# A hybrid diffusion backbone on one core: the decays of its recurrent mixer computed as two exponentials of the tanh

## The chip, the cores and the metric

The kernel runs on 1 core of a Trainium2 chip. TensorE (PE in the rows; its weight load is PEld), VectorE (DVE), ScalarE (ACT), GpSimd (POOL) and SyncE (SP, here a queue for DMAs) each work through their own list of instructions in order and wait for one another through semaphores. The metric is the device time of one execution in microseconds; the median of several runs counts.

## What is computed

One layer over 256 context tokens and 1,024 latent tokens of 1,024 channels: a projection into many column groups, three mixers side by side (a recurrent one over 256 channels, neighbourhood attention over 512, a short gated convolution), an output projection, and an expert mixer that selects 128 of 16,384 rows for each token. The change lies in the recurrent mixer. For each of its two directions `d`:

```
w_raw = w0 + tanh(z_w) @ w_up
decay = exp(-exp(-softplus(-w_raw) - 0.5))          # = exp(-exp(-0.5) * sigmoid(w_raw))
a     = sigmoid(a0 + z_a @ a_up)
b     = kk * a
k_dir = k * (1 + (a - 1) * k_a)
S     = S * decay - (S kk) b^T + v k_dir^T           # token after token
y     = S r
...
out   = (groupnorm(y) * lnx + (sum(r * k * r_k)) * v) * gate
```

The sigmoid is formed from a tanh: sigmoid(x) = 0.5 + 0.5 tanh(x/2).

## The kernel before

The recurrence is worked in batches of 256 tokens, as four chunks of 64. `batch(step, d)` handles one batch of one direction; there are ten (step 0 to 4, both directions), and each has two halves `h` of 128 channels. So the lines inside `for h in range(2)` run 20 times. A half begins with the projection `wr` on TensorE (L498, L499), forms the decays `de` and their inverses `di` (L502 to L518), runs a running product over each chunk (`pe`, `pi`, L525 and L526), forms the key factors `nb` and `kd` (L530 to L532), multiplies them with the inverse decays on GpSimd (`bb`, `kb`, L541 and L542), and starts its matrix products (`p1`, `p2`, L554). Behind the two halves of a batch come a triangular solve (`lp`, `lt`, `lx`, L613 to L630) and the products over the four chunks (`mc`, `yc`, L661 to L680). In the last four batches that complete a group of tokens (`last`), the sum of both directions is normalised (L692 to L707), a bonus is added (`yd`, L713), and the result goes to DRAM as `d_y` (L718). The Ln and Exp of that normalisation stand in `rsqrt` (L136, L137).

The decays before are a chain: tanh on ScalarE, an affine form on VectorE, a second tanh `q`, its squares on ScalarE, three instructions on VectorE, and two products on GpSimd. With q = tanh of a quarter of the exponent, (1 + q)^2 and (1 - q)^2 times (1 + q^2)(1 + q^4)(1 + q^8) give the two exponentials.

A scheduler sets the order of instructions on each engine from the program order and a simulated time; the projections of the attention and convolution inputs (`pj`) and the attention of the first 256 tokens (`attend` with two blocks, L854) depend on nothing in the mixer and are laid between its batches. Tiles with one buffer (`th`, `x2`, `de` and others, tag and `bufs=1`) are reused by the next half, and 128x512 banks of PSUM with the tag `ra` rotate over three buffers. The stretch ends when the mixer's last batch, (4, 1), has written its `d_y`: `group(0, ...)` (L1211) reads it for the output projection.

Of the kernel before, what the change touches and what calls it, by code (L numbers as in the profile page):

```python
# [10 lines left out]
F32 = mybir.dt.float32  # L11
# [4 lines left out]
AF = mybir.ActivationFunctionType  # L16
OP = mybir.AluOpType
AX = mybir.AxisListType

P = 128  # L20
# [8 lines left out]
E05 = float(np.exp(np.float32(-0.5)))  # L29
# [24 lines left out]
def hybrid_kernel(ctx: ExitStack, tc: tile.TileContext, A: dict, out: bass.AP, dbg=None):  # L54
    nc = tc.nc
# [67 lines left out]
    def eps_tile(v):  # L123
        if v not in epst:
            epst[v] = const.tile([P, 1], F32, name=f"eps{len(epst)}")
            nc.vector.memset(epst[v], v)
        return epst[v]

    for v_ in (1e-6, 1e-12, 64e-5):
        eps_tile(v_)  # L130
# [154 lines left out]
    kat = cload("kat", [P, 2], A["rw_k_a"])  # L285
# [124 lines left out]
    cw = st_c.enter_context(pool("cw"))  # L410
# [7 lines left out]
    nc.vector.tensor_scalar_mul(hb[:, 0:4], w0t, 0.5)  # L418
    nc.vector.tensor_scalar_mul(hb[:, 4:8], a0t, 0.5)
    d1 = cw.tile([P, 4, 65], F32, name="d1")  # L420
    nc.vector.memset(d1, 0.0)
# [9 lines left out]
    gp = st_g.enter_context(pool("gp"))  # L431
# [17 lines left out]
    def v4(ap):  # L449
        return ap.rearrange("p (c t) -> p c t", t=64)  # L450
# [4 lines left out]
    def batch(step, d):  # L455
        g = 0 if step == 0 else (step if d == 0 else 5 - step)
        c0, t0, lat = 4 * g, 256 * g, g > 0
        last = g in seen
        if lat:
            seen.add(g)  # L460
        if last:
            bo = gp.tile([P, 2, 4], F32, tag="bo", name=f"bo{g}", bufs=2)
            tl = t0 - TC
        S = [None, None]
# [5 lines left out]
        for h in range(2):  # L470
            ci = 2 * d + h

            def gt(name, shape, bufs=1, h=h):
                return gp.tile(shape, F32, tag=name, name=f"{name}_{step}{d}{h}", bufs=bufs)
# [24 lines left out]
            nc.tensor.matmul(pw[:, 256:], aup[:, ci, :], lwt[:, 1, :], start=True, stop=True)  # L499
            th, q, at = gt("th", [P, 256]), gt("q", [P, 256]), gt("at", [P, 256])  # L500
            x2, x4 = gt("x2", [P, 256]), gt("x4", [P, 256])
            nc.scalar.activation(th, pw[:, :256], AF.Tanh, bias=hb[:, ci:ci + 1], scale=0.5)  # L502
            nc.scalar.activation(at, pw[:, 256:], AF.Tanh, bias=hb[:, 4 + ci:5 + ci], scale=0.5)
            nc.vector.tensor_scalar(th, th, -0.25 * E05, -0.25 * E05, op0=OP.mult, op1=OP.add)
            nc.scalar.activation(q, th, AF.Tanh)

            nc.scalar.activation(th, q, AF.Square)
            nc.scalar.activation(x2, th, AF.Square)
            nc.scalar.activation(x4, x2, AF.Square)
            nc.vector.tensor_scalar_add(x4, x4, 1.0)  # L510
            nc.vector.scalar_tensor_tensor(x2, x2, 1.0, x4, op0=OP.add, op1=OP.mult)
            nc.vector.scalar_tensor_tensor(x2, th, 1.0, x2, op0=OP.add, op1=OP.mult)
            nc.scalar.activation(th, q, AF.Square, bias=1.0)
            nc.scalar.activation(x4, q, AF.Square, bias=1.0, scale=-1.0)
            de, di = gt("de", [P, 4, 65]), gt("di", [P, 4, 65])
            for t_, o_ in ((th, de), (x4, di)):
                nc.gpsimd.memset(o_[:, :, 64 * d:64 * d + 1], 0.0)
                nc.gpsimd.tensor_mul(o_[:, :, 1 - d:65 - d], v4(t_), v4(x2))  # L518
            nc.vector.tensor_scalar(at, at, 0.5, 0.5, op0=OP.mult, op1=OP.add)
            at = v4(at)  # L520

# [6 lines left out]
            tot = pe[:, :, 64:65] if d == 0 else pe[:, :, 0:1]  # L528
            nb, kd = v4(gt("x2", [P, 256])), v4(gt("x4", [P, 256]))
            nc.vector.scalar_tensor_tensor(nb, kk, -1.0, at, op0=OP.mult, op1=OP.mult)  # L530
            nc.vector.tensor_scalar(kd, at, -1.0, kat[:, h:h + 1], op0=OP.add, op1=OP.mult)
            nc.vector.scalar_tensor_tensor(kd, kd, 1.0, kr_, op0=OP.add, op1=OP.mult)  # L532
            krd = gt("krd", [P, 4, 3, 64], 4)
# [34 lines left out]

            ex = v4(gt("q", [P, 256]))
            nc.vector.tensor_mul(ex, p1v[:, :, 1, :], cst[:, C_X0 if d == 0 else C_X1, 0:64].unsqueeze(1).to_broadcast([P, 4, 64]))  # L570
# [110 lines left out]
        if not lat:  # L681
            return
        y = gp.tile([P, 2, 4, 64], F32, tag="y", name=f"y{step}{d}", bufs=1)
        src = ych.rearrange("p (h c b) -> p h c b", h=2, c=4)
# [19 lines left out]
        nc.vector.tensor_reduce(va, y2, op=OP.add, axis=AX.X)  # L704
        rsqrt(gp, rs, va, 8, 64e-5, 1.0 / 64, "gn")
        nc.vector.tensor_mul(y, y, bc(rs))
        nc.vector.tensor_mul(y, y, lnx.unsqueeze(2).to_broadcast([P, 2, 4, 64]))  # L707
        for h in range(2):
            yd = rot("yd", [P, 4, P], 1)
            for a in range(2):  # L710
                q_ = slice(64 * a, 64 * a + 64)
                for u in range(4):
                    nc.vector.scalar_tensor_tensor(yd[q_, u, q_], S[h]["vS"][q_, u], bo[q_, h, u:u + 1], y[q_, h, u], op0=OP.mult, op1=OP.add)  # L713
            ps = bank(f"yo{h}{g}", "ch")
            for u in range(4):
                nc.tensor.matmul(ps[:, u * 64:(u + 1) * 64], yd[:, u, :], cst[:, C_STK, 0:64], start=True, stop=True)
            nc.vector.tensor_mul(gs[:, h, :], ps[:, :256], gs[:, h, :])
# [772 lines left out]
```

## Time and profile before

| | |
|---|---|
| median of 3 runs | 3760.8 us |
| the runs | 3756.59, 3760.8, 3775.57 us |
| the profiled execution's own time | 3766.3 us |
| its span in the trace | 3764.6 us |
| TensorE, busy share of the span | 90% |
| VectorE | 79% |
| ScalarE | 42% |
| GpSimd | 40% |
| first tanh of the mixer's decays (L502) | starts at 143.1 us |
| last write of the mixer's result (L718) | issued at 953.1 us |

The times are for the whole layer. The mixer stands between about 100 and 953 us; the rest of the span is the attention of the later tokens and the expert mixer. Shares over the span say little about this stretch, which has to be read by windows.

### The profile page before, as it was taken

The page shows a single profiled execution, that of the slowest core. Times are in us where ns is not written, and L with a number is a line of the kernel's source. Part 1 is how long each engine was busy: PE and PEld are TensorE (multiplying, and loading weights), DVE is VectorE, ACT ScalarE, POOL GpSimd, SP SyncE. Part 2 cuts the span into 40 slices and gives each one's busy share as a digit, 9 for nine tenths or more (in the row PEclk, how much of TensorE's full clock was granted, in tenths as well). Part 3 has the DMA queues.
Part 4 walks back from the last instruction along what each step waited for, and adds up shares of the span by engine and source line. Part 5 has one row for each costly group of instructions (what it writes and reads, how often), then busy time and mean ns, then how long its engine had stood idle before and what let it go on. Part 6 is the DMA issues. An engine that isn't in the chain of part 4 may idle for free.

```text
span 3764.6 us, 56051 instructions
## 1 busy us (share of the span) xinstructions
PE 3383.9 (90%) x19927; PEld 3052.6 (81%) x19927; DVE 2984.7 (79%) x6392; ACT 1587.2 (42%) x3084; POOL 1503.7 (40%) x1196
## 2 busy tenths in 40 slices
PE   7778888988779887989889999999996999999997
PEld 6567778887668766879889999999985888888886
DVE  6576757886595656978869999999876788888888
ACT  3543333442435433345343776666632333323332
POOL 2444443320044223355433425555451444444443
PEclk9889998998789888999999999999998999999998
DMA  6434534220565645698967879999998999999997
GB/s 245 138 94 147 167 114 121 70 61 22 159 205 171 205 146 174 242 322 295 326 232 263 301 253 358 351 361 357 340 367 272 314 356 348 344 347 333 338 355 244
DMA packets 405784, 928.09 MB, mean 247 GB/s; under 512 B 45568, under 2 KB 182144, under 8 KB 399872
## 3 DMA queue, kind: packets, MB, share of 16 engines
q1 hardware_dynamic: 248064, 408.81, 33.6%
q0 software_dynamic: 111920, 407.95, 30.1%
q10 hardware_dynamic: 45520, 107.76, 7.4%
q8 instruction: 157, 2.57, 0.3%
q14 instruction: 123, 1.01, 0.1%
HBM read 802.74 MB, written 121.63 MB: 246 GB/s over the span
## 4 chain that ended last, share of the span: by engine, by line
PE 39%; DVE 10%; issue 6%; DMA 4%; ACT 2%; POOL 1%; SPq 0%; DVEq 0%; ACTq 0%; POOLq 0%
PE ds L159 5%; PE ds L157 5%; PE ds L158 5%; PE dp L158 5%; PE dp L159 5%; PE dp L157 5%; DVE ru L1159 3%; PE gm L1074 3%; PE dq L157 2%; PE dq L159 2%; PE dq L158 2%; DMA rv<-in_peer_v_dram,idx 2%; DVE acc L1170 1%; DMA kd<-d_kn 1%; DVE ob L1066 1%
## 5 line engine op out<-in xcount | busy, mean ns | idle before, releaser
L1142 POOL DMA_INDIRECT ru<-in_peer_u_dram,idx x384 | 514.5, 1340 | 736.3 <-ACT dqs L1394 168.4
L1142 POOL DMA_INDIRECT rv<-in_peer_v_dram,idx x384 | 511.6, 1332 | 707.1 <-ACT dqs L1394 272.2
L1159 DVE CUSTOM_DVE_ANT_0 ru<-ru,h 128x1024 f32<-128x1024 f32 x384 | 475.7, 1254 | 82.4 <-DMA ru<-in_peer_u_dram,idx 80.2
L1170 DVE SCALAR_TENSOR_TENSOR acc<-rv,gw,acc 128x1024 f32<-128x1024 f32 x381 | 488.2, 1281 | 49.5 <-DMA rv<-in_peer_v_dram,idx 44.4
L158 PE MATMUL dp<-dvls,dwhs 128*128 128x512 f32 x896 | 348.2, 389 | 0.0
L159 PE MATMUL dp<-dvhs,dwls 128*128 128x512 f32 x896 | 346.1, 389 | 0.0
L157 PE MATMUL dp<-dvhs,dwhs 128*128 128x512 f32 x896 | 318.7, 394 | 4.7 <-ACT dvhs L1344 4.7
L207 POOL TENSOR_TENSOR wl<-w,wh 128x1024 fp32r<-128x1024 f32 x68 | 170.3, 2507 | 291.8 <-ACT wh L205 268.3
L157 PE MATMUL pj<-hbh,wh 128*128 128x512 f32 (+1 forms) x544 | 220.8, 407 | 24.8 <-ACT wh L205 15.9
L1276 ACT ACTIVATE ge<-ds 128x256 f32<-128x256 f32 (+1 forms) x256 | 110.8, 434 | 265.3 <-PE ds L159 224.4
L159 PE MATMUL pj<-hbh,wl 128*128 128x512 f32 (+1 forms) x544 | 215.7, 397 | 2.7 <-POOL wl L207 2.7
L158 PE MATMUL pj<-hbl,wh 128*128 128x512 f32 (+1 forms) x544 | 216.8, 399 | 0.8 <-POOL hbl L188 0.8
L1348 ACT CAST dwhs<-dws 128x640 fp32r<-128x640 f32 x128 | 91.6, 730 | 269.3 <-DVE dws L1347 141.6
L157 PEld LDWEIGHTS dp<-dvhs,dwhs 128*128 128x128 f32 x896 | 171.1, 191 | 40.8 <-ACT dvhs L1344 5.1
L158 PEld LDWEIGHTS dp<-dvls,dwhs 128*128 128x128 f32 x896 | 168.2, 188 | 34.9
L159 PEld LDWEIGHTS dp<-dvhs,dwls 128*128 128x128 f32 x896 | 168.2, 188 | 34.8
L157 PE MATMUL dq<-dvhs,dwhs 128*128 128x512 f32 x384 | 150.8, 393 | 31.5 <-ACT dvhs L1344 28.7
L1345 DVE TENSOR_TENSOR dvls<-dvs,dvhs 128x1024 fp32r<-128x1024 f32 x128 | 155.5, 1219 | 24.2 <-ACT dvhs L1344 23.8
L1344 ACT CAST dvhs<-dvs 128x1024 fp32r<-128x1024 f32 x128 | 133.0, 1051 | 76.5 <-DMA dvs<-in_peer_v_dram 76.4
L1074 PE MATMUL gm<-oa,ob 128*128 128x128 f32 x1280 | 158.2, 276 | 3.2 <-DVE oa L1061 1.9
L1394 ACT COPY dqs<-dq 128x512 f32<-128x512 f32 x90 | 52.8, 587 | 256.5 <-PE dq L159 256.5
L1074 PEld LDWEIGHTS gm<-oa,ob 128*128 128x128 f32 x1280 | 153.6, 193 | 4.2 <-issue 4.1
(1995 smaller groups left out, 10488.4 us busy)
## 6 DMA issues: line engine op xcount, KB each, us to landing
du<-in_peer_ut_dram SPq DMA_DIRECT2D x128, 512.0 KB
dvs<-in_peer_v_dram SPq DMA_DIRECT2D x128, 512.0 KB
d_ge<-ge ACTq DMA_DIRECT2D x128, 320.0 KB
d_g<-gt ACTq DMA_DIRECT2D x40, 1024.0 KB
dgs<-d_g SPq DMA_DIRECT2D x32, 1280.0 KB
dws<-d_ge SPq DMA_DIRECT2D x128, 320.0 KB
w<-in_w_in_dram SPq DMA_DIRECT2D x68, 512.0 KB
wq<-in_q_w_dram SPq DMA_DIRECT2D x48, 512.0 KB
```

Source lines behind the costliest of these rows:

```text
L157: nc.tensor.matmul(ps, lh_, rh_, start=start, stop=False)
L158: nc.tensor.matmul(ps, lh_, rl_, start=False, stop=False)
L159: nc.tensor.matmul(ps, ll_, rh_, start=False, stop=stop)
L207: WE[0].tensor_tensor(wl, w, wh.bitcast(F32), op=OP.subtract)
L1074: nc.tensor.matmul(ps[:, t * P:(t + 1) * P], ob[:, q + t], oa[:, q + t], start=True, stop=True)
L1142: paced(nc.gpsimd.indirect_dma_start(out=r, out_offset=None, in_=A[tab], in_offset=bass.IndirectOffsetOnAxis(ap=idx[:, tt, s:s + 1], axis=0)))
L1159: yield from rows("peer_u", tt, lambda s, u: nc.vector.tensor_tensor_reduce(u, u, h2, 1.0, 0.0, OP.mult, OP.add, act[:, s:s + 1]))
L1170: nc.vector.scalar_tensor_tensor(acc, v, w[:, s:s + 1], acc, op0=OP.mult, op1=OP.add)
L1276: ev = nc.scalar.activation(ge[:, t0:t0 + n], ps, AF.Gelu_apprx_tanh)
L1344: nc.scalar.copy(vh, v)
L1345: sv = nc.vector.tensor_tensor(vl, v, vh.bitcast(F32), op=OP.subtract)
L1348: nc.scalar.copy(wh, wt)
```

## The change

The decays become two exponentials of the first tanh: exp(-c) and exp(+c) with c = 0.5 exp(-0.5) (1 + tanh), each one ScalarE instruction that writes straight into `de` and `di`. The factor -a becomes one affine form on ScalarE (`nb`, from the tanh `at`), the factor 1 + (a - 1) k_a another (`kd`, with scale and bias per channel from the new small tile `kac`), and VectorE multiplies each with `kk` and `k`. The tile `q` is gone; the temporary `ex` takes the buffer of `th` instead. In the finishing batches the bonus product `vb` = v times its sum is formed before the normalised `y` is there, the reciprocal root comes from `rsqrt_few` (twelve small VectorE instructions, no table functions), and `yd` is a plain sum over four chunks at a time.

```diff
-    for v_ in (1e-6, 1e-12, 64e-5):
+    for v_ in (1e-6, 1e-12, 64e-5, -0.5 * E05, 0.5 * E05, -0.5):
         eps_tile(v_)
...
+    kac = cw.tile([P, 2, 2], F32, name="kac")
+    nc.vector.tensor_scalar_mul(kac[:, 0], kat, 0.5)
+    nc.vector.tensor_scalar(kac[:, 1], kat, -0.5, 1.0, op0=OP.mult, op1=OP.add)
...
-            th, q, at = gt("th", [P, 256]), gt("q", [P, 256]), gt("at", [P, 256])
-            x2, x4 = gt("x2", [P, 256]), gt("x4", [P, 256])
+            th, at = gt("th", [P, 256]), gt("at", [P, 256])
+            nb, kd = gt("x2", [P, 256]), gt("x4", [P, 256])
             nc.scalar.activation(th, pw[:, :256], AF.Tanh, bias=hb[:, ci:ci + 1], scale=0.5)
+            de, di = gt("de", [P, 4, 65]), gt("di", [P, 4, 65])
+            for sg, o_ in ((-1.0, de), (1.0, di)):
+                nc.gpsimd.memset(o_[:, :, 64 * d:64 * d + 1], 0.0)
+                nc.scalar.activation(o_[:, :, 1 - d:65 - d], v4(th), AF.Exp, bias=eps_tile(sg * 0.5 * E05), scale=sg * 0.5 * E05)
             nc.scalar.activation(at, pw[:, 256:], AF.Tanh, bias=hb[:, 4 + ci:5 + ci], scale=0.5)
-            nc.vector.tensor_scalar(th, th, -0.25 * E05, -0.25 * E05, op0=OP.mult, op1=OP.add)
-            nc.scalar.activation(q, th, AF.Tanh)
-
-            nc.scalar.activation(th, q, AF.Square)
-            nc.scalar.activation(x2, th, AF.Square)
-            nc.scalar.activation(x4, x2, AF.Square)
-            nc.vector.tensor_scalar_add(x4, x4, 1.0)
-            nc.vector.scalar_tensor_tensor(x2, x2, 1.0, x4, op0=OP.add, op1=OP.mult)
-            nc.vector.scalar_tensor_tensor(x2, th, 1.0, x2, op0=OP.add, op1=OP.mult)
-            nc.scalar.activation(th, q, AF.Square, bias=1.0)
-            nc.scalar.activation(x4, q, AF.Square, bias=1.0, scale=-1.0)
-            de, di = gt("de", [P, 4, 65]), gt("di", [P, 4, 65])
-            for t_, o_ in ((th, de), (x4, di)):
-                nc.gpsimd.memset(o_[:, :, 64 * d:64 * d + 1], 0.0)
-                nc.gpsimd.tensor_mul(o_[:, :, 1 - d:65 - d], v4(t_), v4(x2))
-            nc.vector.tensor_scalar(at, at, 0.5, 0.5, op0=OP.mult, op1=OP.add)
-            at = v4(at)
+            nc.scalar.activation(nb, at, AF.Identity, bias=eps_tile(-0.5), scale=-0.5)
+            nc.scalar.activation(kd, at, AF.Identity, bias=kac[:, 1, h:h + 1], scale=kac[:, 0, h:h + 1])
+            nb, kd = v4(nb), v4(kd)
...
-            nb, kd = v4(gt("x2", [P, 256])), v4(gt("x4", [P, 256]))
-            nc.vector.scalar_tensor_tensor(nb, kk, -1.0, at, op0=OP.mult, op1=OP.mult)
-            nc.vector.tensor_scalar(kd, at, -1.0, kat[:, h:h + 1], op0=OP.add, op1=OP.mult)
-            nc.vector.scalar_tensor_tensor(kd, kd, 1.0, kr_, op0=OP.add, op1=OP.mult)
+            nc.vector.tensor_mul(nb, kk, nb)
+            nc.vector.tensor_mul(kd, kd, kr_)
...
-            ex = v4(gt("q", [P, 256]))
+            ex = v4(gt("th", [P, 256]))
...
+        if last:
+            vb = []
+            for h in range(2):
+                vb.append(S[h]["gt"]("vb", [P, 4, 64], 2))
+                nc.vector.tensor_mul(vb[h], S[h]["vS"], bo[:, h].unsqueeze(2).to_broadcast([P, 4, 64]))
...
-        rsqrt(gp, rs, va, 8, 64e-5, 1.0 / 64, "gn")
+        rsqrt_few(gp, rs, va, 8, 64e-5, 1.0 / 64, "gn")
...
-                for u in range(4):
-                    nc.vector.scalar_tensor_tensor(yd[q_, u, q_], S[h]["vS"][q_, u], bo[q_, h, u:u + 1], y[q_, h, u], op0=OP.mult, op1=OP.add)
+                nc.vector.tensor_add(yd[q_, :, q_], vb[h][q_], y[q_, h])
```

With fewer instructions in the mixer the scheduler sets other orders on all engines. Three places follow. The first is ScalarE (ACT) at the last half of the mixer, step 4, direction 1, h = 1; the names end in `411`. Before, eight instructions belong to the decays and the tanh `at` (L502 to L514), with two exponentials and two copies of the attention between them (L823, L824, L835):

```order
L502 ACTIVATE th_411_5837<-wr43_5834,hb_734 128x256
L503 ACTIVATE at_411_5839<-wr43_5834,hb_734 128x256
L505 ACTIVATE q_411_5838<-th_411_5837 128x256
L507 ACTIVATE th_411_5837<-q_411_5838 128x256
L508 ACTIVATE x2_411_5840<-th_411_5837 128x256
L509 ACTIVATE x4_411_5841<-x2_411_5840 128x256
L823 ACTIVATE s71_8081,m271_8082<-pc71_8086,m271_8082 128x256
L824 ACTIVATE s71_8081,m271_8082<-s71_8081,m271_8082 128x512
L514 ACTIVATE x4_411_5841<-q_411_5838 128x256
L835 COPY pT71_8099<-pt710_8100 128x512
L835 COPY pT71_8099<-pt714_8106 128x256
L513 ACTIVATE th_411_5837<-q_411_5838 128x256
```

The same half in the changed kernel (its lines are numbered differently):

```order
L505 ACTIVATE th_411_5596<-wr43_5593,hb_740 128x256
L510 ACTIVATE at_411_5597<-wr43_5593,hb_740 128x256
L509 ACTIVATE de_411_5601<-th_411_5596,eps3_112 128x4x64
L509 ACTIVATE di_411_5602<-th_411_5596,eps4_114 128x4x64
L511 ACTIVATE x2_411_5598<-at_411_5597,eps5_116 128x256
L512 ACTIVATE x4_411_5599<-at_411_5597,kac_743 128x256
L534 COPY kx0_794<-krd_411_5616 64x4x64 x2
```

Six instructions in one run, with no table load between the tanh and the two exponentials.

The second place is TensorE (PE) where the attention of the first 256 tokens ends; `yt300` is its last piece, `p1_43` and `p2_43` open the mixer's last half, `lp_430`, `lt_430` and `lx_430` belong to its last solve, and `yo` is the last product of a finishing batch. Before:

```order
L839 MATMUL po71_8110<-vN30_7929,pT71_8099 128x64 x6
L846 MATMUL yt300_8118<-cst2_95,yn0_7342 128x128
L624 MATMUL lt_401_5533<-XT_400_5470,pm_400_5531 128x128 x4
L618 MATMUL lp_411_5539<-X_401_5486,E_401_5386 128x128 x4
L846 MATMUL yt300_8118<-cst2_95,yn1_7343 128x128
L554 MATMUL p1_43_5884<-krd_411_5870,bb0_794 128x128 x4
L624 MATMUL lt_411_5546<-XT_401_5479,pm_401_5544 128x128 x4
L638 MATMUL x12_400_5553<-rx_400_5284,XT_400_5470 128x192 x2
L554 MATMUL p2_43_5885<-krd_411_5870,kb0_796 128x128 x4
```

In the changed kernel:

```order
L834 MATMUL po71_7855<-vN30_7674,pT71_7844 128x64 x6
L841 MATMUL yt300_7863<-cst2_95,yn0_7087 128x128
L615 MATMUL lt_430_5768<-XT_411_5733,pm_411_5766 128x128 x4
L619 MATMUL lx_430_5773<-pm_411_5766,XT_411_5733 128x128 x4
L841 MATMUL yt300_7863<-cst2_95,yn1_7088 128x128
L711 MATMUL yo04_5454<-cst_734,yd0_4478 128x64 x4
L609 MATMUL lp_421_5780<-X_410_5731,E_410_5539 128x128 x4
L711 MATMUL yo14_5462<-cst_734,yd0_4478 128x64 x4
L615 MATMUL lt_421_5787<-XT_410_5724,pm_410_5785 128x128 x4
```

The attention now ends beside the last solve of the mixer, where before it ended ahead of the last half's products. Counted over the whole list, 278 of the attention's 296 products (each matmul counted singly) stood ahead of the last half's `wr` before, and 200 stand there now; all 1,200 of the projections' products stand ahead of it in both.

The third place is GpSimd (POOL) in step 3, direction 0, h = 1 (`301`), where the two columns of `de` and `di` that start the running product are set to zero; `wl` is the low part of a projection's weight, and its number that of the weight block. In the changed kernel:

```order
L533 TENSOR_TENSOR kb0_792<-x4_211_3690,pi_211_3702 64x4x64 x2
L537 TENSOR_TENSOR bh_211_3717<-bb0_790,pe_211_3701 128x512
L538 TENSOR_TENSOR bh_211_3718<-kb0_792,pe_211_3701 128x512
L207 TENSOR_TENSOR wl14_6829<-w14_6825,wh14_6827 128x1024
L207 TENSOR_TENSOR wl18_6863<-w18_6859,wh18_6861 128x1024
L207 TENSOR_TENSOR wl15_6908<-w15_6904,wh15_6906 128x1024
L207 TENSOR_TENSOR wl19_6942<-w19_6938,wh19_6940 128x1024
L508 MEMSET de_301_4136 128x4
L508 MEMSET di_301_4137 128x4
```

Before, the products that fill `de` and `di` stood in this list as well:

```order
L546 TENSOR_TENSOR bh_300_4220<-bb0_794,pe_300_4201 128x512
L547 TENSOR_TENSOR bh_300_4221<-kb0_796,pe_300_4201 128x512
L790 TENSOR_TENSOR kl10_7451<-kd10_7440,kh10_7441 128x768
L790 TENSOR_TENSOR kl20_7553<-kd20_7542,kh20_7543 128x768
L518 TENSOR_TENSOR di_301_4309<-x4_301_4295,x2_301_4294 128x4x64
L518 TENSOR_TENSOR de_301_4308<-th_301_4291,x2_301_4294 128x4x64
```

The products are gone from GpSimd, the memsets are still there, and other large splits stand ahead of them.

## Rows read from the trace of the kernel before

**Rows 1.** Busy time by windows, five stretches up to the last write of the mixer's result. Columns: the stretch and its length in us, busy us and number of instructions of PE, PEld, DVE, ACT and POOL, then the granted TensorE clock as a share of full speed, the busy share of the DMA engines, and GB/s.

```profile
100.00:360.00 260.00, 208.63 (x1040) 169.82 (x1038) 159.97 (x359) 119.32 (x212) 126.92 (x110) 0.90 0.40 127
360.00:620.00 260.00, 225.65 (x1399) 201.82 (x1400) 170.51 (x366) 83.47 (x179) 109.92 (x97) 0.95 0.45 137
620.00:871.00 251.00, 224.43 (x1635) 213.63 (x1633) 218.84 (x695) 114.70 (x294) 70.86 (x89) 0.91 0.25 72
871.00:914.00 43.00, 36.50 (x226) 33.91 (x226) 32.89 (x111) 11.35 (x25) 5.40 (x38) 0.80 0.05 16
914.00:953.50 39.50, 25.27 (x172) 22.92 (x170) 17.27 (x44) 7.11 (x16) 0.00 (x0) 0.85 0.03 8
```

**Rows 2.** What TensorE waited for between 100 and 620 us, the largest waits for VectorE: total us, times, longest us.

```profile
PE lt L624 <- DVE pm L620: 16.1, 5, 6.1
...
PE pr L649 <- DVE pr L653: 9.5, 4, 3.4
...
PE lp L618 <- DVE X L629: 6.3, 2, 4.5
```

**Rows 3.** Three instants of the last half, from the timelines of ScalarE, VectorE and TensorE (start us, duration us, instruction, and in brackets the idle time before it): its first tanh, its scan of the inverse decays, its first product. Below them the last piece of the attention on TensorE.

```profile
861.11 0.47 ACT L502 ACTIVATE th<-wr,hb 128x256 f32<-128x256 f32 x1 [2.39 <-PE wr L499]
867.36 1.14 DVE L526 TENSOR_TENSOR_SCAN pi<-di,d 128x260 f32<-128x260 f32 x1
872.23 1.13 PE L554 MATMUL p<-krd,bb 128*128 128x128 f32 x8 [1.21 <-DVE krd L536]
...
870.69 0.33 PE L846 MATMUL yt<-cst,yn 128*128 128x128 f32 x1 [0.78 <-DVE yn L840]
```

**Rows 4.** Groups of VectorE by line and shape between 100 and 960 us: names, shapes, count, then busy us in total and mean ns of one, and the idle time before them.

```profile
L504 DVE TENSOR_SCALAR th<-th 128x256 f32<-128x256 f32 x20 | 7.1, 357 | 30.6 <-ACT th L502 30.5
L510 DVE TENSOR_SCALAR x<-x 128x256 f32<-128x256 f32 x20 | 8.7, 435 | 7.3 <-ACT x L509 6.9
L511 DVE SCALAR_TENSOR_TENSOR x<-x,x 128x256 f32<-128x256 f32 x20 | 10.8, 541 | 0.4
L512 DVE SCALAR_TENSOR_TENSOR x<-th,x 128x256 f32<-128x256 f32 x20 | 8.4, 419 | 0.3
L519 DVE TENSOR_SCALAR at<-at 128x256 f32<-128x256 f32 x20 | 5.8, 288 | 0.4
L531 DVE TENSOR_SCALAR x<-at,kat 128x256 f32<-128x256 f32 x20 | 7.0, 350 | 0.0
L530 DVE SCALAR_TENSOR_TENSOR x<-kkc,at 128x256 f32<-128x256 f32 x20 | 12.6, 629 | 0.0
L532 DVE SCALAR_TENSOR_TENSOR x<-x,kc 128x256 f32<-128x256 f32 x20 | 15.1, 754 | 0.0
L713 DVE SCALAR_TENSOR_TENSOR yd<-vS,bo,y 64x64 f32<-64x64 f32 x64 | 16.0, 280 | 1.2 <-PE yo L716 0.2
L653 DVE TENSOR_TENSOR pr<-pr,krd 64x256 f32<-64x256 f32 x64 | 26.9, 421 | 5.7 <-PE pr L649 4.7
```

**Rows 5.** The first tanh of each half (L502) by windows: how many halves start in a stretch. Columns: the stretch, its length, busy us of ACT and count, clock, DMA share, GB/s.

```profile
100.00:360.00 260.00, 3.32 (x7) 0.90 0.40 127
360.00:620.00 260.00, 2.38 (x5) 0.95 0.45 137
620.00:871.00 251.00, 3.81 (x8) 0.91 0.25 72
```

**Rows 6.** Instructions of ScalarE: groups of the first and second tanh between 100 and 960 us (columns as in rows 4), and from one line's view an Identity with a scale and a bias per partition (durations min/median/max in ns).

```profile
L502 ACT ACTIVATE th<-wr,hb 128x256 f32<-128x256 f32 x20 | 9.5, 476 | 16.9 <-PE wr L499 16.9
L505 ACT ACTIVATE q<-th 128x256 f32<-128x256 f32 x20 | 8.5, 427 | 16.5 <-DVE th L504 16.5
L930 ACT ACTIVATE x<-x,modT,sc x24: 585/595/824, 1003.8 to 1944.6; 128x256 f32<-128x256 f32 x16, 128x512 f32<-128x512 f32 x8
```

**Rows 7.** Groups of GpSimd between 100 and 960 us, columns as in rows 4: the weight splits and the products that fill `di` and `de`.

```profile
L207 POOL TENSOR_TENSOR wl<-w,wh 128x1024 fp32r<-128x1024 f32 x42 | 105.2, 2505 | 202.0 <-ACT wh L205 179.8 <-PE pj L159 10.8 <-PE lt L624 10.6
...
L518 POOL TENSOR_TENSOR di<-x,x 128x256 f32<-128x256 f32 x20 | 16.5, 824 | 128.0 <-DVE x L512 80.2 <-ACT pT L835 27.3 <-DVE yb L597 15.6
```

**Rows 8.** The timeline of VectorE and TensorE in the last 13 us of the mixer (start us, duration us, engine, line; in brackets the idle time before): the normalisation, `yd`, the last products and the last multiplication before the write. The last row is the same product in an earlier batch.

```profile
940.85 0.69 DVE L704 TENSOR_REDUCE st<-ysq 128x8 f32<-128x512 f32 x1 [0.69 <-ACT ysq L703]
944.22 0.17 DVE L139 SCALAR_TENSOR_TENSOR gnt<-st,gnt 128x8 f32<-128x8 f32 x1 [2.69 <-ACT gnt L138]
944.83 0.69 DVE L706 TENSOR_TENSOR y<-y,st 128x512 f32<-128x512 f32 x1
946.28 1.79 DVE L713 SCALAR_TENSOR_TENSOR yd<-vS,bo,y 64x64 f32<-64x64 f32 x8
948.31 1.85 DVE L713 SCALAR_TENSOR_TENSOR yd<-vS,bo,y 64x64 f32<-64x64 f32 x6 [0.24 <-PE yo L716]
952.67 0.42 DVE L717 TENSOR_TENSOR gs<-yo,gs 128x256 f32<-128x256 f32 x1 [1.56 <-PE yo L716]
...
947.61 1.94 PE L716 MATMUL yo<-cst,yd 128*128 128x64 f32 x8 [9.83 <-DVE yd L713]
950.66 1.97 PE L716 MATMUL yo<-cst,yd 128*128 128x64 f32 x8 [1.12 <-DVE gs L717]
...
854.51 1.00 PE L716 MATMUL yo<-cst,yd 128*128 128x64 f32 x8
```

**Rows 9.** A buffer's reuse in the timelines of VectorE and ScalarE: the sum over the temporary `ex` of one half (L571), and the first tanh of the half after it.

```profile
616.17 0.58 DVE L571 TENSOR_REDUCE E<-q 128x64 f32<-128x256 f32 x1
...
625.20 0.48 ACT L502 ACTIVATE th<-wr,hb 128x256 f32<-128x256 f32 x1 [0.44 <-PE wr L499]
```

## The prediction

> **What bounds the kernel now.** I read the windows first, since shares over the whole span say nothing about the mixer. In [rows 1] TensorE is busy for most of every stretch up to 871 us, and VectorE, slack at first (160.0 of 260 us), reaches 218.8 of 251 us between 620 and 871. There the two engines bound the work together: TensorE idles 26.6 us of 251 and VectorE 32.2. Behind 871 us nothing but the mixer is left, and TensorE idles 6.5 of 43 and 14.2 of 39.5 us. With 51.4 and 34.4 us in the first two stretches this is 133 us of TensorE idle time between 100 and 953.5 us. The matrix work of the stretch stays, so a gain can come only from this idle time and from the granted clock. The second view is what TensorE waits for [rows 2]: early on, its largest waits are for VectorE's work on the solve (`pm`, `pr`, `X`), 31.9 us in three rows. VectorE is not short of time there (330.5 busy of 520 us); it is late because its list holds other things first. The third view is one half's own length [rows 3]: from the first tanh to the scan `pi` 6.3 us, to the first product 11.1 us. Twenty halves follow one another, since buffers and the `ra` banks pass from half to half.
>
> **The change, part by part.** *VectorE.* Six instructions of each half go (L504, L510, L511, L512, L519, L531): 7.1 + 8.7 + 10.8 + 8.4 + 5.8 + 7.0 = 47.8 us over 20 halves, 2.39 us each [rows 4]. L530 and L532 become plain products; the rows have none of this exact form, and between the 421 ns of a smaller sum (L653) and their own 629 and 754 ns I take their own, that is no gain. The bonus: 64 pieces of 280 ns (16.0 us in this window) become 16 sums of some 421 ns (6.7 us) and 8 products `vb` of some 629 ns (5.0 us). The root goes from three small instructions to twelve, 9 more in each of four batches, at 0.20 us from start to start (944.22 to 944.83 holds three [rows 8]): 7.2 us. These two cancel within 3 us. VectorE loses about 45 us.
>
> *GpSimd* loses two products a half, 16.5 us for `di` alone [rows 7]; it is not what others mostly wait for, so I book nothing. The memsets stay.
>
> *ScalarE.* A half goes from eight instructions of about 0.42 to 0.48 us to six: two tanh, two exponentials and one Identity at about 0.48 (the price of L502, which also has a bias per partition) and one Identity at 0.595 [rows 6], some 0.5 us less. ScalarE is busy less than half the time [rows 1]; nothing is booked. Its two Identity forms replace L519 and L531, which cost 288 and 350 ns on VectorE against about 476 and 595 here. The Trainium skill, page "ScalarE: Activation LUTs", section "Rules for kernel authors", says that additions and multiplications belong on VectorE, not ScalarE. By that rule, with the rows' own durations, the move would lose 0.43 us a half, 8.7 us in all, and the sum below would be 19 instead of 28. I do not follow it: these two are needed only when both scans are done, and VectorE is the engine with more work.
>
> *The length of a half.* From the first tanh two ScalarE instructions and a scan of some 0.7 us now lead to the second scan: 0.476 + 0.476 + 0.7 = 1.7 us in place of 6.3 [rows 3, 6], 4.6 us less per half. That alone would be 92 us over 20 halves, but TensorE's and VectorE's work has to fit, so I don't add it; it lets the scheduler lay the mixer earlier beside the other work. The order shows it: at the last half's `wr` 200 instead of 278 of the 296 attention products stand ahead, and the attention now ends beside the last solve.
>
> *New waits.* The first tanh takes its buffer `th` back from `ex` of the half before, so it waits for the sum L571, and the attention's copies and the weight casts queue behind it on ScalarE. Now this sum is over 8.4 us before the next tanh [rows 9], and it still has to come for p1 and the banks, so I book nothing. The scan waits for the memsets on GpSimd, which is a rival below.
>
> *The sum, by stretch.*
> 1. Tail, 914 to 953.5. From the end of L704 (941.54) to L706 (944.83) pass 3.29 us; twelve small instructions take 2.4, so 0.9 less. Then yd (two sums, 0.84), yo, gs (0.42), yd (0.84), yo, gs (0.42): with 1.0 us for a yo, as in an earlier batch, this ends 4.5 us after the start of yd, with its recorded 1.95 us 6.4; before it was 946.28 to 953.09, 6.8. So 0.9 + 0.4 to 0.9 + 2.3, that is 1.3 to 3.2 [rows 8]. I take 3, since the recorded yo includes waits for pieces of `yd`.
> 2. 871 to 914. This ran after the attention's last piece (870.69 [rows 3]); now attention lies beside it. Idle 6.5 us, and the clock: granted 0.80, a mix of 2.4 and 1.2 GHz, against 0.91 in the stretch before; 36.5 x (1 - 0.80/0.91) = 4.4. At most 11; I take 8.
> 3. 620 to 871. Eight halves start here [rows 5]: 8 x 2.39 = 19 us less on VectorE, 1 us more for finishing, 18. TensorE is close behind as a bound, so half: 9.
> 4. 100 to 620. Twelve halves, 29 us less on a VectorE with slack. Of the 31.9 us in which TensorE waits for it [rows 2] I take a quarter, 8, because those waits depend on the order in VectorE's list and its load falls by a tenth.
>
> Together 28 us. The profiled execution's own time, 3766.3, becomes 3738; it lies 5.5 above the median of the runs, and from that the forecast is 3760.8 - 28 = **3733 us**. Behind the mixer everything starts relative to its end, so I carry the gain through; the order there differs little, and five table loads fewer in its order, at the attention and the gelu, are booked at zero.
>
> **Bounds.** Smallest: only the tail at 1.3 us, 3759. Largest: 3.2 + 11 + 18 + 31.9 = 64 us, 3697.
>
> **Rivals.**
> - *TensorE is the bound already.* The gain in front is eaten because the projections and the attention still have to pass through TensorE, and only the tail and a part of stretch 2 count, 3 to 8 us: 3755 us, within 0.5%. For it: 87 to 89% busy from 360 to 871 us [rows 1]. Against it: 61 us idle there, of which VectorE is the cause in many rows.
> - *The chain of halves bounds.* If the order was set by a half's length, most of the 92 us comes, up to the idle time that is not needed by start and tail, 65 us: 3695 us. For it: 20 halves that follow one another; against it: that TensorE would then run without a gap.
> - *Slower: the memsets on GpSimd hold the scans.* The third place of the order shows four weight splits ahead of them. One split takes 2.505 us, and its idle time in front is 202.0 / 42 = 4.8 us [rows 7], so a run of four is 29 us. The price falls due when a half's tanh comes before its memset; from two such halves on (58 us) the forecast's 28 is gone and the kernel is slower, with two 3760.8 - 28 + 58 = 3791 us. For it: halves that come earlier meet more projection splits in GpSimd's list. Against it: before, the products of `di` and `de` stood in the same list, and their longest idle time was for VectorE (80.2 of 128.0 us), not for splits [rows 7].
>
> **How the numbers follow.** The forecast's case (15 to 50 us less) gets 0.60, the first rival 0.20, the second 0.12, the third 0.08. About 0.5%, 19 us, is what a measurement of this kernel can tell from no change: the runs shown spread by 19 us. Of the forecast's case about 0.08 lies between 15 and 19 us. So faster is 0.52 + 0.12 + a little for a first rival with more in front, 0.66; same 0.26; slower 0.08. The range goes from 3692, inside the second rival, to 3760, past the first one.
>
> **What would show it.** Right: VectorE's busy time between 100 us and the last `d_y` down by about 45 us; the last `d_y` issued at about 925 instead of 953.1 us; first tanh to `pi` near 2 us in quiet halves; TensorE's idle time up to there about 105 us instead of 133; the clock above 0.80 in the last 80 us; no table loads between tanh and exponentials. Wrong: GpSimd's memsets naming a split or a ScalarE cast before a late scan; the first tanh waiting for L571's successor; or an end of the mixer that comes earlier while the total does not follow, which would mean that the stretches behind it give the gain back.

## The result: 46 us faster where 28 were forecast

The changed kernel takes 3712.2 us (median of 6 runs, 3700.6 to 3716.4) against 3758.6 of the kernel before: 46 us less between the medians. The ratio is 0.9861, 95% interval 0.9847 to 0.9874, which of 3758.6 is 52 us (47 to 58); the experiments below go by such ratios. The direction was right and the time lies inside the range; the size was not, since the forecast was 28 us. The profiled execution took 3700.6 us, the fastest of the six.

The head of the page of after: its span, then busy time of each engine.

```profile
span 3698.8 us, 55802 instructions
PE 3353.5 (91%) x19927; PEld 3027.9 (82%) x19927; DVE 2932.3 (79%) x6273; ACT 1549.2 (42%) x3017; POOL 1472.0 (40%) x1156
```

Busy time by windows of after, stretches that answer to [rows 1]; the last ends with the last `d_y`, issued at 908.1 us instead of 953.1. Columns as there.

```profile
100.00:360.00 260.00, 224.94 (x1193) 190.14 (x1192) 157.52 (x374) 120.83 (x220) 119.66 (x111) 0.91 0.44 136
360.00:620.00 260.00, 235.54 (x1460) 211.78 (x1461) 161.95 (x366) 81.34 (x170) 97.65 (x80) 0.94 0.43 131
620.00:829.00 209.00, 180.58 (x1329) 169.54 (x1329) 173.51 (x531) 83.58 (x216) 57.74 (x102) 0.92 0.28 77
829.00:869.00 40.00, 37.03 (x295) 34.77 (x295) 30.93 (x130) 14.64 (x41) 0.00 (x0) 1.00 0.11 31
869.00:908.50 39.50, 27.09 (x192) 24.99 (x190) 19.14 (x48) 4.20 (x12) 0.00 (x0) 0.83 0.08 24
```

TensorE's idle time in them is 35.1, 24.5, 28.4, 3.0 and 12.4 us, together 103 instead of 133. Ahead of 620 us it fell by 26 us, behind by 4.

VectorE's groups of after between 100 and 910 us, columns as in [rows 4]: the two scans, the two plain products, the sums of `yd`, the products `vb`.

```profile
L518 DVE TENSOR_TENSOR_SCAN pe<-de,d 128x260 f32<-128x260 f32 x20 | 15.5, 776 | 16.7 <-ACT de L509 16.7
L519 DVE TENSOR_TENSOR_SCAN pi<-di,d 128x260 f32<-128x260 f32 x20 | 15.0, 748 | 0.0
L523 DVE TENSOR_TENSOR x<-x,kc 128x256 f32<-128x256 f32 x20 | 10.4, 518 | 0.0
L522 DVE TENSOR_TENSOR x<-kkc,x 128x256 f32<-128x256 f32 x20 | 9.0, 448 | 0.0
L708 DVE TENSOR_TENSOR yd<-vb,y 64x256 f32<-64x256 f32 x16 | 6.6, 415 | 0.2
L678 DVE TENSOR_TENSOR vb<-vS,bo 128x256 f32<-128x256 f32 x8 | 3.3, 418 | 2.4 <-DMA vS<-d_v 2.4
```

The first half in the timelines of after: from the start of the tanh to that of the second scan 2.6 us, where the half in [rows 3] had 6.3. Added over the 20 halves, this length was 192 us before and is 69 now.

```profile
139.82 0.48 ACT L505 ACTIVATE th<-wr,hb 128x256 f32<-128x256 f32 x1
140.54 0.52 ACT L509 ACTIVATE de<-th,eps 128x256 f32<-128x256 f32 x1
140.94 0.52 ACT L509 ACTIVATE di<-th,eps 128x256 f32<-128x256 f32 x1
...
142.38 0.67 DVE L519 TENSOR_TENSOR_SCAN pi<-di,d 128x260 f32<-128x260 f32 x1
```

The end of the mixer in after, against [rows 8]: the last sum of squares, the root done, `yd`, the products, the last multiplication.

```profile
896.74 0.69 DVE L700 TENSOR_REDUCE st<-ysq 128x8 f32<-128x512 f32 x1 [0.69 <-ACT ysq L699]
...
899.89 0.69 DVE L702 TENSOR_TENSOR y<-y,st 128x512 f32<-128x512 f32 x1
...
901.34 0.87 DVE L708 TENSOR_TENSOR yd<-vb,y 64x256 f32<-64x256 f32 x2
902.35 1.94 PE L711 MATMUL yo<-cst,yd 128*128 128x64 f32 x8 [8.69 <-DVE yd L708]
...
907.66 0.42 DVE L712 TENSOR_TENSOR gs<-yo,gs 128x256 f32<-128x256 f32 x1 [2.12 <-PE yo L711]
```

### The profile page after: what moved, and what is told of

It is laid out like the page before. It is cut to its first block, busy times and chain, and to the rows that moved or that the text cites. A ratio compares the mean times of both kernels' runs of the same rounds, so it can differ in the third digit from the quotient of the medians.

```text
span 3698.8 us, 55802 instructions
## 1 busy us (share of the span) xinstructions
PE 3353.5 (91%) x19927; PEld 3027.9 (82%) x19927; DVE 2932.3 (79%) x6273; ACT 1549.2 (42%) x3017; POOL 1472.0 (40%) x1156
## 4 chain that ended last, share of the span: by engine, by line
PE 39%; DVE 11%; DMA 6%; issue 5%; ACT 1%; POOL 1%; SPq 0%; DVEq 0%; ACTq 0%; POOLq 0%
PE dp L157 5%; PE dp L159 5%; PE dp L158 5%; PE ds L159 5%; PE ds L157 4%; PE ds L158 4%; DVE ru L1154 3%; PE gm L1069 2%; PE dq L157 2%; PE dq L158 2%; PE dq L159 2%; DMA ru<-in_peer_u_dram,idx 1%; DMA qd<-d_q 1%; DMA du<-in_peer_ut_dram 1%; DMA rv<-in_peer_v_dram,idx 1%
## 5 line engine op out<-in xcount | busy, mean ns | idle before, releaser
L1343 ACT CAST dwhs<-dws 128x640 fp32r<-128x640 f32 x128 | 91.6, 730 | 270.6 <-DVE dws L1342 138.9
L158 PEld LDWEIGHTS dp<-dvls,dwhs 128*128 128x128 f32 x896 | 168.5, 188 | 35.1
L159 PEld LDWEIGHTS dp<-dvhs,dwls 128*128 128x128 f32 x896 | 168.4, 188 | 35.1
L1340 DVE TENSOR_TENSOR dvls<-dvs,dvhs 128x1024 fp32r<-128x1024 f32 x128 | 155.6, 1220 | 20.7 <-ACT dvhs L1339 20.4
```

Source lines behind the costliest of these rows:

```text
L158: nc.tensor.matmul(ps, lh_, rl_, start=False, stop=False)
L159: nc.tensor.matmul(ps, ll_, rh_, start=False, stop=stop)
L1340: sv = nc.vector.tensor_tensor(vl, v, vh.bitcast(F32), op=OP.subtract)
L1343: nc.scalar.copy(wh, wt)
```

## Experiments

Every kernel here computes the whole result. "Front" is the stretch from 100 us to the last `d_y`, "behind" the rest of the profiled span. Ratios are to the kernel before, on the same chip, and gains in us are worked out from them where nothing else is said; one profile each.

| kernel | ratio (95%) | VectorE busy, front | TensorE idle, front | last `d_y` | behind |
|---|---|---|---|---|---|
| before | 1 | 599.2 | 132.7 | 953.1 | 2811.5 |
| e5_control | 1.0004 (0.9992-1.0015) | 591.0 | 132.0 | 939.7 | 2811.5 |
| after | 0.9861 (0.9847-0.9874) | 542.8 | 103.0 | 908.1 | 2790.7 |
| e1_decays | 0.9839 (0.9815-0.9862) | 564.3 | 111.3 | 921.0 | 2788.8 |
| e3_affine | 0.9900 (0.9883-0.9918) | 586.7 | 126.9 | 932.7 | 2786.1 |
| e2_tail | 0.9952 (0.9937-0.9967) | 596.6 | 130.2 | 940.4 | 2795.3 |
| e10_root | 0.9927 (0.9908-0.9946) | 602.5 | 129.2 | 943.7 | 2788.1 |
| e11_bonus | 1.0004 (0.9991-1.0017) | 591.0 | 134.7 | 949.2 | 2813.3 |
| e13_old_root | 0.9926 (0.9910-0.9942) | 541.7 | 112.2 | 916.8 | 2799.8 |
| e4_load | 0.9939 (0.9921-0.9957) | 600.5 | 124.7 | 934.6 | 2793.1 |
| e6_length | 0.9847 (0.9824-0.9870) | 538.1 | 113.1 | 914.6 | 2773.9 |
| e12_gpsimd | 0.9847 (0.9831-0.9863) | 550.1 | 112.2 | 909.9 | 2790.8 |
| e8_onescan | 0.9821 (0.9804-0.9838) | 532.8 | 102.4 | 899.6 | 2782.4 |
| e14_root_more | 0.9956 (0.9941-0.9971) | 600.8 | 130.3 | 940.1 | 2799.2 |
| e15_root_tables | 0.9943 (0.9925-0.9961) | 606.1 | 134.5 | 951.8 | 2795.1 |
| e9_one_more | 0.9990 (0.9976-1.0004) | 595.8 | 137.4 | 950.9 | 2799.6 |
| e16_pass_more | 0.9980 (0.9966-0.9994) | 604.8 | 139.8 | 956.1 | 2795.0 |

**One execution's chance.** The control:

```
-Y  = gp.tile([P, 8, 16], ..., bufs=2)
+Y  = gp.tile([P, 8, 16], ..., bufs=1)     (yb the same)
```

> The kernel before with two small VectorE tiles of the solve (Y, yb) in one buffer instead of two, as the tail kernel and the load kernel have them; the instruction order of TensorE, ScalarE, GpSimd and SyncE is the same as before, and VectorE's but for two rows. It shows what a second profile of the same program differs by. If TensorE's busy time of 720 us between 100 us and the last d_y (705 to 710 in the five other profiles) belongs to the order of before, it stays near 720, with a time of 3760; if it is the chance of one execution, it comes out near 710 with a time of 3760 all the same; if the buffers are what the tail kernel gained by, the time is near 3740.

The time is the same. The whole front of the control by windows (columns as in [rows 1]):

```profile
100.00:939.70 839.70, 707.73 (x4463) 631.98 (x4463) 590.98 (x1571) 335.02 (x723) 308.03 (x333) 0.92 0.34 104
```

and the same row of before:

```profile
100.00:953.10 853.10, 720.40 (x4466) 642.02 (x4464) 599.22 (x1572) 335.95 (x724) 313.10 (x334) 0.91 0.34 103
```

Idle time 132.0 and 132.7, behind 2811.5 both times; but the same matmuls were busy 12.7 us longer in the profile that the forecast was built on, and its front ended 13.4 us later. So from one profile the front's end is good to some 13 us only, while the idle time of these two differs by 0.7. Against the control the changed kernel's last `d_y` comes 31.6 us earlier, not 45. The control's single buffers for `Y` and `yb` are also in e2, e4, e11 and e12.

**The parts one by one.** e1 has the new tanh and exponentials in place of L502 to L518 of before, and keeps L519 and the rest; e3 takes over `nb`, `kd` and their two products; e2 the root and `vb`/`yd`; e10 the root, e11 `vb`/`yd`; e13 is the changed kernel with one line back:

```
-rsqrt_few(gp, rs, va, 8, 64e-5, 1.0 / 64, "gn")
+rsqrt(gp, rs, va, 8, 64e-5, 1.0 / 64, "gn")
```

> The kernel before with the decays alone as two exponentials of the tanh; L519, L530 to L532 of before, the root and the pieces of yd stay. VectorE loses four instructions a half (L504, L510, L511, L512, 35.0 us in the rows). Theory A, the time goes by VectorE's work (the whole change took 56 us from VectorE and brought the mixer's end 45 us forward, 0.8 us per us): 0.8 x 35 = 28 us, about 3731. Theory B, the time goes by the length of a half's front (6.3 to about 2 us, all of it in this part): nearly the whole gain, 42 us, about 3716.

> The kernel before with the end of a batch alone changed: the root in twelve small VectorE instructions, vb formed ahead, yd by two sums. Term 1 of the forecast: 3 us, about 3756. Theories A and B: VectorE's work is the same within a few us and the front of a half is untouched, so 0 to 3 us too. If the tail were mis-sized, here is where it shows: 10 us or more, below 3750.

> The kernel before with nb and kd alone as affine forms on ScalarE and one plain product each: VectorE loses L519, L531 and what the two plain products are cheaper by (8 us in the rows of the changed kernel), 21 us in all; the front of a half up to the scans is as before. Theory A: 0.8 x 21 = 17 us, about 3742. Theory B: none, 3759. The forecast's shares (an eighth of its 22 us at VectorE's rate there): about 5 us.

> The kernel before with the root alone in twelve small VectorE instructions (five table loads fewer in the order, as in the tail kernel). Its order differs from before from TensorE's row 1950 on up to the last 3,911 rows. If table loads or the order behind the mixer made the tail kernel's 21 us, it is all here, about 3742; by term 1 of the forecast, 1 us, 3760.

> The kernel before with the bonus product formed ahead alone (vb, and yd by two sums; Y and yb in one buffer to make room). It removes 9 us of VectorE work net in the pieces of yd, but its order is that of before again for the last 13,001 of TensorE's 15,160 rows. If the gain behind belongs to the order: 0 to 2 us, about 3760. If it belongs to the shorter finish: up to 20 us, 3742.

> The changed kernel with the root as before (three passes of ScalarE with their table loads, three instructions of VectorE). Its order is that of before again for the last 11,593 of TensorE's 15,160 rows. If the root (its work or the order that comes with it) is worth 25 us behind the mixer here too, about 3737, with the front as short as in the changed kernel; if the front alone makes the 46 us, 3712.

In time the parts give 61 us (decays), 38 (affine), 27 (root) and none (bonus): 126 together, where the whole gives 52; root and bonus in one kernel, e2, give 18 (12 to 24). In the front's idle time the parts add up, against the control: 20.7 + 5.1 + 2.8 - 2.7 = 26, and the whole 29. The three small terms are no surer than that: e9 and e16 below, which take no work away, idle 5 and 8 us more in the front than the control. What doesn't add up lies behind: e1, e3 and e10 are each 23 to 25 us shorter there than the control, and the whole only 21. That gain can be had once. e13 shows what the root is worth in the changed kernel: with the old root 28 us are gained (22 to 34), so the root carries 24 of the 52 (18 of the 46 between the medians), in the profiles 9 in the front and 9 behind. Up to 757 us the two kernels have the same order of matmuls, and TensorE idles 78.6 and 81.0 us from 100 to 750; so most of the 9 in the front come with the finishing batches.

**Load, length, GpSimd.** e4 puts VectorE work back beside the chain, e6 length without VectorE work, e12 GpSimd's products:

```
+nc.vector.tensor_mul(v4(zz), kd, inv)                     (e4, behind kd's product)
+for _ in range(5): nc.vector.tensor_scalar(zz, zz, 0.5, 0.5, op0=OP.mult, op1=OP.add)
+for _ in range(10): nc.scalar.activation(th, th, AF.Identity)   (e6, behind the tanh)
+nc.gpsimd.tensor_mul(o_[...], v4(t_), one)                (e12, behind each exponential)
```

> The changed kernel with VectorE work put back beside the chain: in each half, behind kd's product, one product and five affine passes over a scratch tile that nobody reads, about 2 us a half, 40 us in all; the front of a half stays short. Theory A: 0.8 x 40 = 32 us of the 46 are lost, about 3744. Theory B: nothing is lost, 3712.

> The changed kernel with ten passes of ScalarE over th, one after the other, between the tanh and the two exponentials: the front of a half is as long as before again (first tanh to pi about 6 us), VectorE's work stays short, ScalarE gets 84 us more. Theory A (VectorE's work): near the changed kernel, 3712. Theory B (length of the front): most of the gain is lost, about 3750.

> The changed kernel with GpSimd's two products a half put back between the exponentials and the scans (a product by 1 into de and di), some 32 us of GpSimd work in all and 1.6 us more in the front of a half; Y and yb in one buffer to make room. If only VectorE's work counts in the front: TensorE idle about 103 us before the last d_y, and 3712. If GpSimd's work counts (its busy time fell by 38 us): idle back up by 10 or more, about 3725 to 3740.

e4: VectorE was busy 57.7 us more than in the changed kernel (the passes came out dearer than expected), TensorE idled 21.7 us more and the time rose by 24 us between the medians, 29 by the ratios: 0.4 to 0.5 us per us. Theory A's 0.8 is refuted, the load itself is not. In e6 it is 10 us now from the tanh to `pi`, here in the first half:

```profile
139.35 0.48 ACT L505 ACTIVATE th<-wr,hb 128x256 f32<-128x256 f32 x1
...
149.44 0.67 DVE L521 TENSOR_TENSOR_SCAN pi<-di,d 128x260 f32<-128x260 f32 x1
```

Added over the 20 halves, this length is 247 us in e6, 55 more than before the change, yet TensorE idles in the front only 10 us more than in the changed kernel, and 19 less than in the control. The time is no worse, though the part behind, 17 us shorter than in the changed kernel, has a share in that. Theory B falls: the length of a half does not set the time; 178 us more of it cost at most these 10. e12, with GpSimd's work back, idles 9 us more in the front and is no slower than the changed kernel either.

**One scan.** e8 sums the logarithms with one scan and takes both exponentials behind it:

```
-two memsets, two Exp of th, two scans (pe, pi)
+nc.scalar.activation(de[...], v4(th), AF.Identity, bias=1.0)
+nc.vector.tensor_tensor_scan(fl(lg), d1, fl(de), 0.0, OP.mult, OP.add)    (d1: 0 at a chunk's start, else 1)
+nc.scalar.activation(pe, lg, AF.Exp, scale=-0.5 * E05); nc.scalar.activation(pi, lg, AF.Exp, scale=0.5 * E05)
```

> The changed kernel with one scan a half instead of two: ScalarE adds 1 to the tanh, VectorE sums it along the chunk (one scan), and ScalarE's two exponentials of the sum give pe and pi directly; one memset fewer. VectorE loses 20 scans of 0.75 us, 15 us; the front of a half is as long as in the changed kernel, ScalarE gets one instruction a half more. Theory A: 0.8 x 15 = 12 us faster, about 3700. Theory B: no gain, 3712.

67 us faster than before, at 3692.9 the fastest version: faster than the changed kernel by the two intervals. The front's idle time is that of the changed kernel (102.4); its last `d_y` comes 8 us sooner, and its part behind is 8 us shorter. Each is less than the 13 us between the control's front and that of before, so where its 15 us against the changed kernel come from is not shown.

**What is gained behind.** e9 adds one small instruction to each finishing batch, e16 a pass of 512 columns there, e14 the instruction of e9 to e10, e15 the old root's three ScalarE passes to e10:

```
+nc.vector.tensor_scalar(mu, rs, 0.5, 0.5, op0=OP.mult, op1=OP.add)        (e9, e14)
+nc.vector.tensor_scalar(y, y, 1.0, 0.0, op0=OP.mult, op1=OP.add)          (e16)
+three nc.scalar.activation on mu: Ln of va, Exp, Square; result unread    (e15)
```

> The kernel before with one VectorE instruction of 8 columns more in each of the four finishing batches (its result is read by nobody): no work is taken away. The scheduler's order is the same up to row 2080 of TensorE's list, that is through the mixer's front, and another one behind, up to the last 3,911 rows. If the gain behind the mixer (10 to 20 us in every profile whose order differs from before, none in the control with the order of before) belongs to the order, this kernel gains it too, about 3745, with no TensorE idle time less before the last d_y (132). If it belongs to the work that the change removes, it stays at 3761.

> The kernel with the new root alone and one VectorE instruction of 8 columns more in each finishing batch, which gives TensorE's list another order behind its row 1950. If the 26 us of the root belong to its work, they stay, about 3734; if they belong to the one order it happened to get, they move by 10 us or more, towards 3760.

> The kernel with the new root alone, and the three passes of ScalarE of the old root (logarithm, exponential, square, with their table loads) put back beside it: they run on the same input, and nobody waits for what they give. If ScalarE's passes and table loads cost the 26 us, about 3760; if the chain through them did, or the order, about 3734.

> The kernel before with one VectorE pass of 512 columns more in each finishing batch, about 0.55 us four times, on the path to the last d_y. No work is taken away; the order is another one from TensorE's row 1950 to the last 3,911 rows. If another order by itself gains behind the mixer, about 3745; if not, 3762.

e15 keeps 21 of the root's 27 us, its interval overlapping e10's, and all its matmuls stand in e10's order: most of what the root saves is not ScalarE's passes and table loads. e14, in another order, keeps 16 (11 to 22). Two kernels without less work, e9 and e16, are 12 and 16.5 us shorter behind in their profiles; of that e9 shows 4 us in time, not told from none, and e16 7.5 (2 to 13); in the front they idle 5 and 8 us more.

The order can be seen at work. I cut the spans where 13,100 and where 3,850 of the program's matmuls are still to start. This piece lies behind the mixer and holds the same matmuls in all kernels. Their order in it is that of before in the control, e11 and e13; e10, e12 and e15 have that of the changed kernel. Columns as in [rows 1], for before, e13, after, e10 and e16:

```profile
1365.10:2825.30 1460.20, 1368.63 (x9251) 1318.62 (x9251) 1268.76 (x2926) 754.59 (x1571) 646.26 (x480) 0.97 0.83 299
1318.10:2775.40 1457.30, 1366.41 (x9251) 1316.26 (x9250) 1268.64 (x2927) 753.61 (x1571) 642.49 (x481) 0.97 0.84 299
1309.50:2755.80 1446.30, 1367.78 (x9251) 1321.01 (x9250) 1273.14 (x2926) 746.74 (x1566) 647.30 (x480) 0.97 0.84 300
1347.80:2790.40 1442.60, 1366.22 (x9252) 1320.36 (x9251) 1272.83 (x2926) 747.03 (x1566) 639.13 (x480) 0.98 0.84 301
1372.10:2809.70 1437.60, 1360.88 (x9251) 1315.33 (x9250) 1269.07 (x2927) 755.29 (x1571) 647.14 (x481) 0.98 0.84 303
```

TensorE idled in it 90.0 to 91.6 us in the four kernels with the order of before, and 74.1 to 81.2 in the thirteen others. e13, with the decays of the changed kernel, idles as before; e10, with the decays of before, as the changed kernel; and e16, from which nothing was removed, idles 76.7. Nor does the gain need fewer table loads: e16 has all 47 of before in this piece, the changed kernel 42. What TensorE waited for late in it, in the control (2658.4 to 2813.3 us):

```profile
PE ds L157 <- ACT du119h L1085: 2.1, 1, 2.1
PE ds L159 <- DVE du117l L1087: 2.0, 1, 2.0
PE gm L1074 <- DVE oa L1061: 1.9, 1, 1.9
PE ds L157 <- ACT du123h L1085: 1.5, 1, 1.5
PE ds L157 <- ACT du125h L1085: 1.5, 1, 1.5
PE ds L157 <- ACT du112h L1085: 1.0, 1, 1.0
```

the same in e13, whose decays are those of the changed kernel (2620 to 2776 us),

```profile
PE ds L157 <- ACT du119h L1080: 2.1, 1, 2.1
PE ds L159 <- DVE du117l L1082: 2.0, 1, 2.0
PE gm L1069 <- DVE oa L1056: 1.9, 1, 1.9
PE ds L157 <- ACT du125h L1080: 1.5, 1, 1.5
PE ds L157 <- ACT du123h L1080: 1.5, 1, 1.5
PE ds L157 <- ACT du112h L1080: 1.0, 1, 1.0
```

and in the changed kernel (2608.6 to 2758.1 us).

```profile
PE ds L157 <- ACT du122h L1080: 2.1, 1, 2.1
PE ds L157 <- ACT du115h L1080: 1.0, 1, 1.0
PE ds L159 <- DVE du111l L1082: 0.9, 1, 0.9
PE ds L157 <- ACT du111h L1080: 0.6, 1, 0.6
PE ds L157 <- ACT du119h L1080: 0.6, 1, 0.6
```

e10 has the waits of the changed kernel. So these waits for the weight splits `du` go with the order of the instructions, to a tenth of a us, and not with what was removed 1,700 us earlier.

Front and behind together account for most of the times. A kernel's lower idle time in the front plus its shorter part behind, against the control, is 7 us for e9, 9 for e16, 26 for e10, 32 for e13 and 50 for the whole, where the ratios give 4, 7.5, 27, 28 and 52; for e1 and e12 it falls 17 us short.

## Why the prediction was right and wrong

- **What bounds.** Right. TensorE's idle time in the front was to fall from 133 to about 105 us; it fell to 103.0.
- **VectorE, 45 us less.** 48.2 against the control. Within it L530 and L532, for which I took their own price, became products of 448 and 518 ns: 8.3 us more than booked. The bonus (none in e11) and GpSimd (e12, no slower) were rightly booked at zero.
- **Term 1, the tail, 3 us.** 0.9. The root's 3.29 us became 2.46 as worked out, but from `yd` to the last `d_y` it took 6.8 us as before: a yo there is 1.94 us with both sums done, so its recorded length before held no wait for pieces of `yd`: the long reading of the two (6.4) was the right one.
- **Terms 2 to 4, 25 us.** By the idle time of the first two stretches (26 us) and of the rest (4), the early stretch was sized too small and the late one too large. The share of a half per us of VectorE work, used behind 620 us, is near e4's 0.4; the whole front gave 0.6. The clock granted in the last 80 us was 1.00 and 0.83 where it had been 0.80 and 0.85, as the prediction's signs had it; but TensorE's busy time in the whole front is only 2.6 us below the control's, where term 2 held 4.4 for the clock.
- **The Identity forms on ScalarE.** With their two products alone (e3) they gain 38 us and lose nothing: TensorE's idle time in the front falls by 5 us, and the rest lies behind, where e16 gains without them. By the Trainium skill, page "ScalarE: Activation LUTs", section "Rules for kernel authors", which gives additions and products to VectorE, they should have lost; the measurement decides. Instruction by instruction the trace agrees with the rule (0.52 and 0.60 us on ScalarE, 0.29 and 0.35 on VectorE). That VectorE's fuller list outweighed this is argued, not shown apart.
- **The rivals.** "The chain of halves bounds" is refuted by e6, "TensorE is the bound already" by the idle time. The memsets held no scan: L518 waits for ScalarE's exponentials alone (16.7 us). The wait of the first tanh for `ex` did not show.
- **The step that failed** is "Behind the mixer everything starts relative to its end, so I carry the gain through; the order there differs little", and with it the root, booked with the bonus at nothing, its table loads at zero. The part behind fell by 21 us in the profiles. Its order did differ: only the last 3,910 of TensorE's matmuls stand in the order of before, and in the piece above TensorE idles 78.5 us in the new order, 91.6 in the old. The root brings that order (e10 has it, e13 has not). It carries 24 of the 52 us (18 of the 46 between the medians), and without it the kernel gains 28, the number forecast; that agreement is partly chance, since 12 of e13's us lie behind in its profile.

What stays open: why the order of before costs TensorE 9 to 17 us more in that piece than every other order tried; and whether e1 alone beats the whole change (61 against 52 us, intervals that overlap).

## What to carry to other kernels

Where a scheduler orders the whole program, a change at one place moves waits far behind it; before booking the part behind at zero, compare its order, and test each part alone and the whole without it, since such gains don't add. A kernel that adds a little work and so gets another order (here e16) shows how much of a gain needs no work removed. Price removed work by the idle time of the engine that bounds, not by a landmark of one profile: here the landmark moved by 13 us between two executions of one order, the idle time by 0.7. In this kernel VectorE's work was worth 0.4 to 0.6 us per us, the length of the chain at most 10 us of idle time for 178.

## What the runs showed of the hardware

The same matmuls in the same order took 720.4 and 707.7 us of busy time in two executions (granted clock 0.91 and 0.92), with 132.7 and 132.0 us of idle time. VectorE's affine pass over 128x256, 288 to 357 ns in [rows 4], took 674 ns on average in e4:

```profile
L527 DVE TENSOR_SCALAR zz<-zz 128x256 f32<-128x256 f32 x100 | 67.4, 674 | 1.4
```

The trace tells the two kinds apart. The 34 passes that no GpSimd instruction overlaps took 266 to 295 ns, the 28 that lie wholly beside GpSimd instructions 1,091 on average; the others lie partly beside one. Five beside GpSimd's products, and two with GpSimd idle:

```profile
142.79 4.34 DVE L527 TENSOR_SCALAR zz<-zz 128x256 f32<-128x256 f32 x5
143.38 1.42 POOL L537 TENSOR_TENSOR kb<-x,pi 64x256 f32<-64x256 f32 x2
144.87 1.05 POOL L541 TENSOR_TENSOR bh<-bb,pe 128x512 f32<-128x512 f32 x1
...
845.67 0.27 DVE L527 TENSOR_SCALAR zz<-zz 128x256 f32<-128x256 f32 x1
...
847.74 0.28 DVE L527 TENSOR_SCALAR zz<-zz 128x256 f32<-128x256 f32 x1
```

So what makes the pass dear in e4 comes with GpSimd's work beside it; the chain on one tile alone does not. ScalarE's price for 128x256 goes by the form: 0.42 us for the plain pass of e6, 0.47 to 0.48 for a tanh with a bias tile (L505, L510 of after), 0.51 to 0.52 for an exponential or an Identity with a bias tile (L509, L511), 0.60 for an Identity with a scale and a bias tile (L512).
